# The feed-forward down projection as seven products of halves, with resident weights and stored sums of the gated values

## The chip, the cores and the metric

The kernel runs on one core of one Trainium2 chip, as one program. The metric is the device time of one execution in microseconds (us). Matrix products run on TensorE (PE; its weight loads are PEld), elementwise work on VectorE (DVE), ScalarE (ACT) and GpSimd (POOL); all DMAs of this kernel are issued by SyncE (SP). Each engine works through its own instructions in the order in which they were built, and waits on semaphores for the others.

## The reference, cut to what matters

Two layers; the part that the change touches is the feed-forward block of each (1024 tokens, D_MODEL 1024, D_FF 2816 = 22 x 128).

```python
def conv_ffn(x, w_gate, w_up, conv_w, conv_b, w_down):
    a = x @ w_gate
    u = x @ w_up
    ap = jnp.pad(a, ((0, 0), (pad, pad), (0, 0)))
    c = conv_b
    for j in range(CONV_WIDTH):
        c = c + conv_w[j] * ap[:, j:j + S]
    return (jax.nn.gelu(c) * u) @ w_down
...
        f = conv_ffn(x, ffn_w_gate[i], ffn_w_up[i], ...)
        x = layer_norm(ALPHA * x + f, ln_ffn_g[i], ln_ffn_b[i])
        x = x + jax.nn.sigmoid(x @ ple_w_gate[i]) * (p[i] @ ple_w_proj[i])
```

All of it is float32. The kernel splits each factor of a product into a high part (rounded to the PE's input type) and a low part (the rest), and adds three matmuls: high by high, low by high, high by low (`mm3`). One such matmul has a stationary operand of 128 x 128 and a moving one of 128 x 512.

## The kernel before

Tokens are held in two halves: the even ones in tiles 0 to 3, the odd ones in tiles 4 to 7, of 128 each. In a layer, the feed-forward block has two stages.

**Gate and up.** `Products` computes x @ w_gate (even m) and x @ w_up (odd m) for two blocks of 128 columns at a time, f and f + 11, so that m runs from 0 to 21 and a pair of m gives the gated values of two blocks. Each m is already made of seven products of halves (`ORDER`), of 12 matmuls each. VectorE makes the low parts of the weights (line 141) and their sums (318), adds the products up (1167), does the convolution (1236) and multiplies gate by up (1242, `times`). `spill` stores the gated block f (128 x 1024 tokens) in DRAM.

**Down.** `load(n)` fetches one block of w_down and one of the gated values, 512 KB each, and splits both: POOL rounds the weights (138), ACT the gated values (324), VectorE makes the low parts (141). `down` takes two blocks at a time (`GRP`), and for each of the 8 token tiles and 2 column halves makes 6 matmuls into a PSUM bank `pd`, which VectorE adds to the residual `xn` in SBUF (1375 the first time, with the factor ALPHA; 1378 later). That is 22 x 8 x 2 x 3 = 1056 matmuls in a layer.

```python
for n in range(0, NF, GRP):
    ...
    down([ready.pop(a) for a in range(n, n + GRP)], n == 0, before)
```

During the last two blocks `Embedding.load` brings in and splits the weights of the next matmul (`wgh`, `wgl`; low parts on VectorE and POOL in turn, line 148), normalises the first token tiles (lines 891 to 903) and turns tile 0 with 8 transposes; then the matmuls `pg` of line 158 to 160 begin.

The order on each engine is made when the program is built: a scheduler places instructions by its own estimate, within what the data, the tile buffers and some pins allow. Buffers: `unit`/`runit` come from a pool of 36 of 4 KB a partition, `rtile` from 6 of a region, `raw` from 2.

Of the kernel before, what the change touches and what calls it, by code (L numbers as in the profile page):

```python
# [8 lines left out]
F32 = mybir.dt.float32  # L9
# [3 lines left out]
ALU = mybir.AluOpType  # L13
AX = mybir.AxisListType

P = 128
# [11 lines left out]
GRP = 2  # L28
# [3 lines left out]
def tile_hybrid_encoder(  # L32
# [232 lines left out]
    gated = [dr.tile([NF, P, 1024], F32, name=f"gated{i}") for i in range(2)]  # L265
# [831 lines left out]

    class Weights:
# [123 lines left out]
    def ffn(i, w, xt, late, prefetch):  # L1222
# [21 lines left out]
        def spill(n, f):  # L1244
            nc.sync.dma_start(out=gated[i][f], in_=late_c[0][:, n, :])

        def use(pr, m, name):
# [7 lines left out]
            else:  # L1255
                if name == ("c00" if f else "c01"):
                    times(0, 0, pr.c00)
                if name == "c10":
                    times(1, 0, pr.c10)
                    times(1, 1, pr.c11)  # L1260
                    spill(1, f + nh)
                if name == "c01":
                    times(0, 1, pr.c01)
                    spill(0, f)
# [7 lines left out]

        xns = []
        fs = [f for p in range(nh) for f in (p, p + nh)]
        ready = {}

        def load(n):
            f = fs[n]
            out = []
            for dram, hi in ((w_down[i, f], nc.gpsimd), (gated[i][f], nc.scalar)):  # L1280
                v = unit("dr", [P, 1024]) if n < 2 * GRP else region[0].raw("dr", [P, 1024])
                nc.sync.dma_start(out=v, in_=dram)
                h, l = runit("dh", [P, 1024]), runit("dl", [P, 1024])
                split_value(v, h, l, hi)
                out += [h, l]
            ready[n] = out

        def before_down(j):

            if j in (0, 1):  # L1290
                load(j)
            if j in (2, 3):
                for t in range(4 * (j - 2), 4 * (j - 2) + 4):
                    xns.append(unit("xn", [P, 1024]))
                    nc.sync.dma_start(out=xns[t], in_=xmid[i][t])
            if j in (4, 5):
                load(j - 2)
# [10 lines left out]
        for n, (m, name) in enumerate(order):  # L1308
# [50 lines left out]
            if m == NF - 1:  # L1359
                before_down(Products.ORDER.index(name))  # L1360
        finished(len(order) - 1)


        def down(group, first, before=None):
            for t in range(NT):
                if before:
                    before(t)
                for n in range(2):
                    sl = slice(512 * n, 512 * n + 512)
                    po = bank("pd")  # L1370
                    for a, (wh, wl, gh, gl) in enumerate(group):
                        mm3(po, gh[:, t * P:(t + 1) * P], gl[:, t * P:(t + 1) * P], wh[:, sl], wl[:, sl],
                            a == 0, a == len(group) - 1)
                    if first:
                        nc.vector.scalar_tensor_tensor(xns[t][:, sl], xns[t][:, sl], ALPHA, po,
                                                       op0=ALU.mult, op1=ALU.add)
                    else:
                        nc.vector.tensor_tensor(xns[t][:, sl], xns[t][:, sl], po, op=ALU.add)  # L1378

        yield xns  # L1380
        before = None
        for n in range(0, NF, GRP):
            for a in range(n + 2 * GRP, n + 3 * GRP):
                if a < NF:
                    load(a)
            if n + GRP >= NF:
                before = prefetch()
            down([ready.pop(a) for a in range(n, n + GRP)], n == 0, before)


    class Embedding:
# [4 lines left out]
        def load(self):  # L1396

            for k in range(NK):
# [4 lines left out]
            def before(t):  # L1403
                if t == 2:
                    self.stats(0, False)
# [170 lines left out]
```

## Time and profile before

| | |
|---|---|
| median of 3 runs | 3108.19 us (3105.83 to 3110.84) |
| the profiled execution | 3106.23 us, its span 3104.4 us |
| PE busy | 3008.3 us (97%), mean granted clock 0.994 of full speed |
| DVE, ACT, POOL busy | 2280.5, 1186.8, 1022.9 us (73%, 38%, 33%) |
| DMA | 237.5 MB, 77 GB/s over the span |

Engines overlap, so busy times don't add up to the span. A busy time of PE counts a matmul from its start to its modelled end, and matmuls overlap in the pipeline: what one costs is read from the distance between two starts. The time beside an instruction of VectorE is likewise longer than the distance between two starts. The profiled execution lies 1.8 us outside its span, and 2.0 us under the median.

### The profile page before, as it was taken

How to read it: one execution, taken by the hardware profiler on the slowest of the kernel's cores; microseconds unless marked ns; L12 is line 12 of the kernel's file. 1: busy time of each engine (PE TensorE's matmuls, PEld its weight loads, DVE VectorE, ACT ScalarE, POOL GpSimd, SP SyncE). 2: the span in 40 equal slices, each digit the busy share in tenths (PEclk: the TensorE clock that was granted, in tenths of full speed). 3: DMA queues.
4: the chain of work that ended last, by engine and by line, in shares of the span. 5: the costliest groups of instructions: out<-in, count | busy, mean ns of one | idle time of the engine just before them, and what ended most of it. 6: DMA issues, size and time to landing. Idle time of an engine off the chain costs nothing.

```text
span 3104.4 us, 43067 instructions
## 1 busy us (share of the span) xinstructions
PE 3008.3 (97%) x15720; PEld 2582.7 (83%) x15720; DVE 2280.5 (73%) x3890; ACT 1186.8 (38%) x2538; POOL 1022.9 (33%) x1536
## 2 busy tenths in 40 slices
PE   8999999999899999999999999999998999999999
PEld 7888989887678888888888999998776888878887
DVE  6666487876898887766638777777679888877764
ACT  5555477761232222101225555555413222211111
POOL 4444534333222221101225555554223222211112
PEclk9999999999999999999999999999999999999999
DMA  3000100033222222623111000002431222243321
GB/s 121 28 28 24 33 28 8 25 126 126 85 82 82 82 82 93 220 95 109 55 59 36 32 28 28 28 24 77 156 107 68 82 82 82 82 176 136 103 77 65
DMA packets 89251, 237.52 MB, mean 77 GB/s; under 512 B 9040, under 2 KB 32720, under 8 KB 89040
## 3 DMA queue, kind: packets, MB, share of 16 engines
q1 hardware_dynamic: 89040, 234.76, 22.0%
q8 instruction: 125, 2.05, 0.3%
q14 instruction: 86, 0.70, 0.1%
HBM read 179.15 MB, written 55.57 MB: 76 GB/s over the span
## 4 chain that ended last, share of the span: by engine, by line
PE 79%; DVE 10%; DMA 3%; ACT 2%; issue 2%; POOL 2%; SPq 0%; DVEq 0%; ACTq 0%; POOLq 0%
PE pb L159 6%; PE pb L160 6%; PE pb L158 6%; PE xt L163 5%; PE pd L158 4%; PE pd L159 4%; PE pd L160 4%; PE pp L158 4%; PE pp L160 4%; PE pp L159 4%; PE s L587 4%; PE pa L158 2%; PE pa L160 2%; PE pa L159 2%; PE pg L158 2%
## 5 line engine op out<-in xcount | busy, mean ns | idle before, releaser
L141 DVE TENSOR_TENSOR ptl<-xt,pth 128x512 fp32r<-128x512 f32 (+2 forms) x384 | 239.6, 652 | 60.3 <-ACT pth L398 43.6
L158 PE MATMUL pd<-dh,dh 128*128 128x512 f32 x704 | 274.8, 390 | 3.0 <-DVE xn L1378 2.9
L1378 DVE TENSOR_TENSOR xn<-xn,pd 128x512 f32<-128x512 f32 x320 | 212.5, 683 | 87.9 <-PE pd L160 87.2
L158 PE MATMUL pp<-wh,xth 128*128 128x384 f32 x768 | 266.2, 347 | 9.7 <-ACT wh L145 7.3
L159 PE MATMUL pd<-dl,dh 128*128 128x512 f32 x704 | 274.1, 389 | 0.3 <-DVE dl L141 0.3
L160 PE MATMUL pd<-dh,dl 128*128 128x512 f32 x704 | 273.3, 389 | 0.0
L159 PE MATMUL pp<-wl,xth 128*128 128x384 f32 x768 | 259.0, 337 | 1.9 <-DVE wl L148 1.7
L160 PE MATMUL pp<-wh,xtl 128*128 128x384 f32 x768 | 258.0, 336 | 0.0
L439 ACT ACTIVATE e<-s,nmx 128x1024 f32<-128x1024 f32 x192 | 214.5, 1119 | 81.8 <-DVE nmx L837 59.0
L163 PE MATMUL xt<-ident,e 128*128 128x128 f32 x1440 | 198.8, 275 | 9.9 <-POOL e L739 3.0
L324 ACT CAST w<-ws 128x512 fp32r<-128x512 f32 x132 | 81.3, 621 | 331.6 <-PE pb L160 285.9
L158 PE MATMUL pb<-xt,w 128*128 128x512 f32 x528 | 207.1, 392 | 0.0
L159 PE MATMUL pb<-xt,w 128*128 128x512 f32 x528 | 206.9, 392 | 0.0
L160 PE MATMUL pb<-xt,w 128*128 128x512 f32 x528 | 206.7, 392 | 0.0
L163 PEld LDWEIGHTS xt<-ident,e 128*128 128x128 f32 x1440 | 164.1, 141 | 30.6 <-ACT sq L869 5.8
L138 POOL TENSOR_SCALAR w<-ws 128x512 fp32r<-128x512 f32 x44 | 32.5, 741 | 469.3 <-PE pa L160 419.0
L324 ACT CAST dh<-dr 128x1024 fp32r<-128x1024 f32 x44 | 46.1, 1052 | 335.8 <-DMA dr<-gated 202.1
L141 DVE TENSOR_TENSOR w<-ws,w 128x512 fp32r<-128x512 f32 x176 | 161.0, 918 | 4.5 <-ACT w L324 2.2
L138 POOL TENSOR_SCALAR dh<-dr 128x1024 fp32r<-128x1024 f32 x44 | 46.2, 1052 | 356.1 <-PE pd L159 168.5
L158 PEld LDWEIGHTS pd<-dh,dh 128*128 128x128 f32 x704 | 132.2, 188 | 32.7 <-DVE xn L1378 5.1
L158 PEld LDWEIGHTS pp<-wh,xth 128*128 128x128 f32 x768 | 144.6, 188 | 15.2 <-ACT wh L145 8.1
L159 PEld LDWEIGHTS pd<-dl,dh 128*128 128x128 f32 x704 | 132.2, 188 | 27.7 <-DVE dl L141 0.7
(281 smaller groups left out, 8732.4 us busy)
## 6 DMA issues: line engine op xcount, KB each, us to landing
wf<-in_w_gate_dram SPq DMA_DIRECT2D x44, 512.0 KB, 3.8
wf<-in_w_up_dram SPq DMA_DIRECT2D x44, 512.0 KB, 4.1
gated<-c SPq DMA_DIRECT2D x44, 512.0 KB, 2.8
dr<-in_w_down_dram SPq DMA_DIRECT2D x44, 512.0 KB, 3.2
dr<-gated SPq DMA_DIRECT2D x44, 512.0 KB, 3.5
wr<-in_w_c_dram SPq DMA_DIRECT2D x32, 384.0 KB, 3.3
pes<-peo SPq DMA_DIRECT2D x64, 128.0 KB, 1.9
xmid<-xn SPq DMA_DIRECT2D x16, 512.0 KB, 2.8
```

Of the source, the lines that this page charges most:

```text
L138: nc.gpsimd.tensor_scalar(o, i, 1.0, 1.0, op0=ALU.mult, op1=ALU.mult)
L141: nc.vector.tensor_tensor(lo, src, f32(hi), op=ALU.subtract)
L158: nc.tensor.matmul(o, lhsT=lh, rhs=rh, start=start, stop=False)
L159: nc.tensor.matmul(o, lhsT=lh, rhs=rl, start=False, stop=False)
L160: nc.tensor.matmul(o, lhsT=ll, rhs=rh, start=False, stop=stop)
L163: nc.tensor.transpose(o, in_=i, identity=ident)
L324: nc.scalar.copy(h, v)
L439: nc.scalar.activation(dst, s, AF.Exp, bias=negmax, scale=1.0, accum_out=l)
L587: nc.tensor.matmul(s[:, kh * 512:kh * 512 + 512], lhsT=qt[:, hl, i, :], rhs=self.ks[kh][:, j, :], start=hl == 0, stop=hl == 1)
L1378: nc.vector.tensor_tensor(xns[t][:, sl], xns[t][:, sl], po, op=ALU.add)
```

## The change

It replaces the down projection. The tokens are halved (tiles 0 to 3, 4 to 7), so are the FFN width (blocks f and f + 11) and the output columns (two of 512), and the product of the 2 x 2 halves is made from seven products (`DOWN`) instead of eight. A product sums over 11 blocks for 4 token tiles, into 4 PSUM banks that are kept over the 11 blocks. So there are 77 steps n of 4 x 3 = 12 matmuls, 924 in a layer.

- The gate and up stage also makes the four sums of gated halves (`sums_of_gated`, four passes of VectorE over 128 x 512) for each of the 11 pairs of blocks, and stores seven pieces of 128 x 512 in place of two of 128 x 1024.
- The weights of the down projection are loaded once and stay in 22 units. Their sums are made in place on VectorE (`prep`, `draw`): four passes for each f, 44 in a layer.
- Each step splits one gated piece and one weight piece of 128 x 512 (ACT and POOL the high parts, VectorE the low parts). The gated pieces come through two raw buffers, two pieces a load. The split tiles come from the 6 region buffers, two a step, so three steps stand ready at most; in the seventh product they come from the pool.
- VectorE reads the banks after each product instead of after each two blocks: 28 passes from PSUM, 8 from SBUF and 4 over 1024 columns, in place of 176 from PSUM.
- The splits of the next matmul's weights stand beside the 11 steps of the seventh product.

```diff
+DOWN = ("a00", "s4", "a01", "s2", "s3", "s1", "a11")
+AHEAD = 3
...
+    class Down:
+        B = {"a00": (0, 0), "s4": (1, 1), "a01": (1, 0), "s2": (0, 0), "s3": (1, 1), "s1": (0, 1), "a11": (1, 0)}
...
+        def load_g(self, j):
+            m = min(2, self.n - 2 * j)
+            if m > 0:
+                self.raw[j] = region[0].raw("gr", [P, 2, 512])
+                nc.sync.dma_start(out=self.raw[j][:, 0:m, :],
+                                  in_=gated[self.i][2 * j:2 * j + m].rearrange("n p q -> p n q"))
+        def draw(self, n):
...
+            if q == "s2":
+                add(b00, b11, b00)
+            if q == "s3":
+                add(b10, b10, b00, ALU.subtract)
+        def prep(self, n):
...
+            make = runit if q == "a11" else rtile
+            g, w = make("gd", [P, 2, 512]), make("wd", [P, 2, 512])
+            rg, rw = self.raw[n // 2][:, n % 2, :], self.b(f, self.B[q])
+            nc.scalar.copy(g[:, 0], rg)
+            pool_copy(w[:, 0], rw)
+            lo_part(g[:, 1], rg, g[:, 0])
+            lo_part(w[:, 1], rw, w[:, 0])
+            if q == "s4":
+                add(rw, rw, self.b(f, (0, 1)), ALU.subtract)
+            if q == "a01":
+                add(self.b(f, (0, 1)), self.b(f, (0, 1)), self.b(f, (0, 0)), ALU.subtract)
+            self.op[n] = g, w
+            if n % 2 == 1:
+                self.load_g((n + 3) // 2)
+        def product(self, n, t):
+            q, f = n // self.nh, n % self.nh
+            (g, w), ts = self.op[n], slice(t * P, t * P + P)
+            mm3(self.po[t], g[:, 0, ts], g[:, 1, ts], w[:, 0], w[:, 1], f == 0, f == self.nh - 1)
...
+        def run(self, beside):
+            nh, n_all = self.nh, self.n
+            end = n_all - AHEAD
+            for n in range(n_all):
...
+                if n < end:
+                    for t in range(4):
+                        self.product(n, t)
+                elif n == end:
+                    for t in range(4):
+                        for m in range(end, n_all):
+                            self.product(m, t)
...
+                self.draw(n + AHEAD + 2)
+                for _ in range(2):
+                    if self.todo:
+                        self.todo.pop(0)()
+                self.prep(n + AHEAD)
+                if f == nh - 1 and q < 6:
+                    self.todo += self.read(q)
+                if q == 6 and n < end:
+                    beside(f)
...
-        def spill(n, f):
-            nc.sync.dma_start(out=gated[i][f], in_=late_c[0][:, n, :])
+        def spill(name, f, v):
+            nc.sync.dma_start(out=gated[i][DOWN.index(name) * nh + f], in_=v)
+        def sums_of_gated(pr, f):
...
+            for name, o, a, b, op in (("s1", s1, a10, a11, ALU.add), ("s2", s2, s1, a00, ALU.subtract),
+                                      ("s4", s4, a01, s2, ALU.subtract), ("s3", s3, a00, a10, ALU.subtract)):
+                add(o, a, b, op)
+                spill(name, f, o)
...
+            def beside(n):
+                if n == 0:
+                    self.ln = LN(ln_fg[self.i], ln_fb[self.i])
+                    fetch(0)
+                    fetch(1)
+                if n > 0:
+                    for k in ((0,), (1,), (2,), (3, 4), (5,), (6,), (7,))[n - 1] if n <= 7 else ():
+                        fetch(k + 2)
+                        weight(k)
```

Three places of the order that results. **The first pair of the gate and up stage on VectorE**, layer 0: the end of the first gated blocks (`c`), then the weights (`ws`, `wf`, low parts `w`) and the first read of the next m (`u` from `pa`). Before:

```order
L1167 TENSOR_TENSOR u_10626<-u_10626,pb_10705 128x512
L1242 TENSOR_TENSOR c_10441<-c_10441,c_2502_10552 128x512
L1242 TENSOR_TENSOR c_10441<-c_10441,u_10626 128x512
L318 TENSOR_TENSOR ws_10744<-ws_10744,wf_10590 128x512
L141 TENSOR_TENSOR w_10754<-wf_10590,w_10754 128x512
L318 TENSOR_TENSOR ws_10745<-wf_10590,ws_10744 128x512
L141 TENSOR_TENSOR w_10771<-ws_10744,w_10771 128x512
L141 TENSOR_TENSOR w_10789<-ws_10745,w_10789 128x512
L141 TENSOR_TENSOR w_10806<-ws_10744,w_10806 128x512
L1167 TENSOR_TENSOR u_10774<-m_10757,pa_10731 128x512
```

and now, in the same place:

```order
L1330 TENSOR_TENSOR u_10626<-u_10626,pb_10705 128x512
L1405 TENSOR_TENSOR c_10441<-c_10441,c_2502_10552 128x512
L1405 TENSOR_TENSOR c_10441<-c_10441,u_10626 128x512
L319 TENSOR_TENSOR c_2502_10552<-c_10441 128x512
L319 TENSOR_TENSOR c_2464_10384<-c_10441 128x512
L319 TENSOR_TENSOR u_10626<-c_2502_10552,c_10441 128x512
L319 TENSOR_TENSOR ws_10753<-ws_10753,wf_10590 128x512
L319 TENSOR_TENSOR u_10626<-c_10441,u_10626 128x512
L319 TENSOR_TENSOR ws_10754<-wf_10590,ws_10753 128x512
L142 TENSOR_TENSOR w_10763<-wf_10590,w_10763 128x512
L142 TENSOR_TENSOR w_10780<-ws_10753,w_10780 128x512
```

The four sums of gated halves (line 319 into `c`, `c`, `u`, `u`) stand ahead of the weights and of the next read.

**The middle of the down stage on VectorE.** Before, the low parts `dl` of whole blocks stand between the reads of the banks:

```order
L141 TENSOR_TENSOR dl_13615<-dr_13612,dh_13614 128x1024
L1378 TENSOR_TENSOR xn_13499<-xn_13499,pd_13816 128x512
L141 TENSOR_TENSOR dl_13621<-dr_13618,dh_13620 128x1024
L1378 TENSOR_TENSOR xn_13501<-xn_13501,pd_13824 128x512
L1378 TENSOR_TENSOR xn_13501<-xn_13501,pd_13832 128x512
L1378 TENSOR_TENSOR xn_13517<-xn_13517,pd_13840 128x512
```

Now, from the low parts of step 11 (`wd_13866`, `gd_13865`) to those of step 13:

```order
L142 TENSOR_TENSOR wd_13866<-wd_13683,wd_13866 128x512
L142 TENSOR_TENSOR gd_13865<-gr_13787,gd_13865 128x512
L319 TENSOR_TENSOR wd_13683<-wd_13683,wd_13536 128x512
L319 TENSOR_TENSOR wd_13536<-wd_13536 128x512
L319 TENSOR_TENSOR wd_13536<-wd_13683,wd_13536 128x512
L142 TENSOR_TENSOR gd_13888<-gr_13829,gd_13888 128x512
L142 TENSOR_TENSOR wd_13889<-wd_13705,wd_13889 128x512
L319 TENSOR_TENSOR wd_13705<-wd_13705,wd_13538 128x512
L319 TENSOR_TENSOR wd_13538<-wd_13538 128x512
L142 TENSOR_TENSOR gd_13909<-gr_13829,gd_13909 128x512
L142 TENSOR_TENSOR wd_13910<-wd_13725,wd_13910 128x512
```

The sums of weights (line 319), which the source spreads over four products, stand close together: 39 of the 44 lie between the low parts of step 11 and those of step 28, and 4 reads of banks with them.

**The end of the down stage on POOL.** Before, the four low parts of the next weights follow the last rounding of a down block:

```order
L138 TENSOR_SCALAR dh_14830<-dr_14828 128x1024
L148 TENSOR_TENSOR wgl_15105<-wgr_15102,wgh_15104 128x1024
L148 TENSOR_TENSOR wgl_15117<-wgr_15114,wgh_15116 128x1024
L148 TENSOR_TENSOR wgl_15129<-wgr_15126,wgh_15128 128x1024
L148 TENSOR_TENSOR wgl_15141<-wgr_15138,wgh_15140 128x1024
L895 TENSOR_SCALAR rs_15183<-mv_15182 128x1
```

Now they stand among the last roundings (`wd`, of steps 71 to 76):

```order
L139 TENSOR_SCALAR wd_15141<-wd_13789 128x512
L149 TENSOR_TENSOR wgl_15151<-wgr_15098,wgh_15150 128x1024
L139 TENSOR_SCALAR wd_15169<-wd_13809 128x512
L139 TENSOR_SCALAR wd_15203<-wd_13831 128x512
L149 TENSOR_TENSOR wgl_15213<-wgr_15148,wgh_15212 128x1024
L896 TENSOR_SCALAR rs_15184<-mv_15183 128x1
L897 TENSOR_TENSOR rs_15184<-rs_15184,mhalf 128x1
L139 TENSOR_SCALAR wd_15235<-wd_13851 128x512
L149 TENSOR_TENSOR wgl_15243<-wgr_15210,wgh_15242 128x1024
L139 TENSOR_SCALAR wd_15262<-wd_13874 128x512
L139 TENSOR_SCALAR wd_15294<-wd_13895 128x512
L149 TENSOR_TENSOR wgl_15300<-wgr_15240,wgh_15299 128x1024
```

So the roundings of steps 72, 74 and 75 stand behind one of these passes each.

## Rows read from the trace of the kernel before

**Rows 1.** The page: busy time by engine, and the chain that ended last.

```profile
PE 3008.3 (97%) x15720; PEld 2582.7 (83%) x15720; DVE 2280.5 (73%) x3890; ACT 1186.8 (38%) x2538; POOL 1022.9 (33%) x1536
...
PE 79%; DVE 10%; DMA 3%; ACT 2%; issue 2%; POOL 2%; SPq 0%; DVEq 0%; ACTq 0%; POOLq 0%
```

**Rows 2.** Stretches: length, busy time by engine (instructions), granted clock, DMA share, GB/s.

```profile
845.00:860.00 15.00, 10.72 (x36) 8.43 (x37) 14.38 (x21) 5.56 (x8) 3.26 (x3) 0.67 0.00 1
...
875.00:900.00 25.00, 23.31 (x101) 18.99 (x102) 24.71 (x37) 8.96 (x13) 7.85 (x7) 1.00 0.26 86
960.00:1245.00 285.00, 285.00 (x1246) 232.51 (x1245) 228.17 (x321) 80.55 (x115) 72.53 (x70) 1.00 0.24 85
1245.00:1488.00 243.00, 241.24 (x1065) 198.82 (x1065) 177.12 (x237) 31.74 (x31) 32.07 (x28) 1.00 0.38 131
```

**Rows 3.** PE in order of time, both down stages: start, us, line, names.

```profile
1245.05 0.39 PE L158 MATMUL pd<-dh,dh 128*128 128x512 f32 x1
...
1268.85 0.39 PE L158 MATMUL pd<-dh,dh 128*128 128x512 f32 x1
...
1484.42 1.04 PE L163 MATMUL xt<-ident,xn 128*128 128x128 f32 x8
...
1488.04 0.39 PE L158 MATMUL pg<-wgh,xth 128*128 128x512 f32 x1
...
2760.12 0.39 PE L158 MATMUL pd<-dh,dh 128*128 128x512 f32 x1
...
3003.08 0.39 PE L158 MATMUL pg<-wgh,xth 128*128 128x512 f32 x1
```

**Rows 4.** VectorE in order of time, passes of 128 x 512 that follow each other.

```profile
929.23 0.68 DVE L318 TENSOR_TENSOR ws<-ws,wf 128x512 f32<-128x512 f32 x1
929.94 1.66 DVE L318 TENSOR_TENSOR ws<-wf,ws 128x512 f32<-128x512 f32 x1
...
1239.86 0.68 DVE L1167 TENSOR_TENSOR m<-m,pb 128x512 f32<-128x512 f32 x1
1240.46 0.68 DVE L1167 TENSOR_TENSOR c<-u,pb 128x512 f32<-128x512 f32 x1
```

**Rows 5.** VectorE and POOL in order of time where both work.

```profile
893.71 1.17 POOL L138 TENSOR_SCALAR w<-wf 128x512 fp32r<-128x512 f32 x1 [0.46 <-PE pb L160]
893.72 0.68 DVE L1242 TENSOR_TENSOR c<-c,c 128x512 f32<-128x512 f32 x1
894.32 1.09 DVE L318 TENSOR_TENSOR ws<-ws,wf 128x512 f32<-128x512 f32 x1
895.34 0.67 DVE L1167 TENSOR_TENSOR m<-m,pb 128x512 f32<-128x512 f32 x1
```

**Rows 6.** PE after its waits early in the gate and up stage, layer 0.

```profile
849.28 0.77 PE L158 MATMUL pa<-xb,w 128*128 128x512 f32 x1 [9.17 <-DVE u L1167]
849.84 0.63 PE L159 MATMUL pa<-xb,w 128*128 128x512 f32 x1
850.27 0.63 PE L160 MATMUL pa<-xb,w 128*128 128x512 f32 x1
...
875.51 0.50 PE L158 MATMUL pb<-xb,w 128*128 128x512 f32 x1 [1.41 <-DVE u L1167]
875.85 0.40 PE L159 MATMUL pb<-xb,w 128*128 128x512 f32 x1
```

**Rows 7.** By tile: durations (ns min/median/max) of splits on VectorE and POOL.

```profile
L148 DVE TENSOR_TENSOR wgl<-wgr,wgh x8: 1224/1226/1525, 1427.2 to 2962.0; 128x1024 fp32r<-128x1024 f32 x8
L148 POOL TENSOR_TENSOR wgl<-wgr,wgh x8: 2393/2398/2410, 1429.8 to 2967.1; 128x1024 fp32r<-128x1024 f32 x8
...
L138 POOL TENSOR_SCALAR w<-ws x44: 612/619/2029, 831.1 to 2729.0; 128x512 fp32r<-128x512 f32 x44
```

**Rows 8.** VectorE by line and shape, 825 to 1245 us: busy, mean ns.

```profile
L141 DVE TENSOR_TENSOR w<-ws,w 128x512 fp32r<-128x512 f32 x85 | 78.5, 928 | 1.2 <-POOL w L138 0.5
...
L318 DVE TENSOR_TENSOR ws<-wf,ws 128x512 f32<-128x512 f32 x20 | 21.6, 1078 | 0.6
```

**Rows 9.** DMA issues: KB each, median us from issue to landing.

```profile
dr<-gated SPq DMA_DIRECT2D x44, 512.0 KB, 3.5
```

More of the change, by code (lines that the diff above doesn't have):

```diff
@@ L264, in tile_hybrid_encoder @@
     xmid = [dr.tile([NT, P, 1024], F32, name=f"xmid{i}") for i in range(2)]
-    gated = [dr.tile([NF, P, 1024], F32, name=f"gated{i}") for i in range(2)]
+    gated = [dr.tile([7 * NF // 2, P, 512], F32, name=f"gated{i}") for i in range(2)]
     def transposed(xn, put):
@@ L1098, in tile_hybrid_encoder, with residual @@
+    def residual(i, xns, t):
+        xns.append(unit("xn", [P, 1024]))
+        nc.sync.dma_start(out=xns[t], in_=xmid[i][t])
     class Weights:
@@ L1260, in use @@
                     times(1, 1, pr.c11)
-                    spill(1, f + nh)
+                    spill("a01", f, late_c[0][:, 1, 0:512])
+                    spill("a11", f, late_c[0][:, 1, 512:1024])
                 if name == "c01":
                     times(0, 1, pr.c01)
-                    spill(0, f)
+                if name in ("c01", "c10") and not any(x in ("c01", "c10") for x, _ in pr.sums if x != name):
+                    sums_of_gated(pr, f)
         def finished(n):
@@ L1273, in ffn @@
         xns = []
[L1274 to L1297, printed above, removed]
+        down = Down(i, xns)
         pr = [Products(w[m], xt) for m in range(NF)]
@@ L1359, in ffn @@
             if m == NF - 1:
-                before_down(Products.ORDER.index(name))
+                down.ahead(Products.ORDER.index(name))
         finished(len(order) - 1)
[L1364 to L1378, printed above, removed]
-        yield xns
[L1381 to L1388, printed above, removed]
+        yield xns
+        down.run(prefetch())
     class Embedding:
@@ L1396, in load, with fetch, weight @@
         def load(self):
-            for k in range(NK):
-                self.w.append(load_split(w_ple[self.i, k], [P, 1024], "wg", rtile if k < 3 else runit, nc.scalar,
-                                         nc.gpsimd if k % 2 else nc.vector))
-            self.ln = LN(ln_fg[self.i], ln_fb[self.i])
-            def before(t):
-                if t == 2:
+            raw = {}
+            def fetch(k):
+                if k < NK:
+                    raw[k] = unit("wgr", [P, 1024])
+                    nc.sync.dma_start(out=raw[k], in_=w_ple[self.i, k])
+            def weight(k):
+                make = rtile if k < 3 else runit
+                h, l = make("wgh", [P, 1024]), make("wgl", [P, 1024])
+                split(raw.pop(k), h, l, nc.scalar, nc.gpsimd if k % 2 else nc.vector)
+                self.w.append((h, l))
+            def beside(n):
[7 more added lines that the diff above has]
+                        weight(k)
+                if n == 3:
                     self.stats(0, False)
-                if t == 5:
+                if n == 5:
                     self.apply(0)
-                if t == 6:
+                if n == 6:
                     self.stats(1, False)
-                if t == 7:
+                if n == 7:
                     self.turn(0)
-            return before
+            return beside
         def stats(self, t, pin=True):
```

87 lines of the change are left out of this document (86 added, 1 removed).

## The prediction

> **What bounds the kernel now.** I first read engine shares and the chain of waits. PE is busy 97% of the span and makes up 79% of the chain; VectorE comes next with 73% busy and 10% of the chain [rows 1]. Shares are means, so I then read the two stages that change as stretches. In a steady part of gate and up, PE is busy in all of 285.00 us and VectorE in 228.17; in the down stage of layer 0 PE is busy 241.24 of 243.00 us, VectorE 177.12, the DMA engines .38 of the time, at full granted clock [rows 2]. So the down stage is bound by TensorE's instruction count, with a quarter of VectorE free. The question is whether VectorE, which gets the work that pays for fewer products, still delivers each split tile in time.
>
> The pitch of a matmul comes from the list of starts, not from the 0.39 us beside it: 105 matmuls lie between 1245.05 and 1268.85, so 23.80/105 = 0.2267 us [rows 3]. The down stage lasts 1488.04 − 1245.05 = 242.99 us in layer 0 and 3003.08 − 2760.12 = 242.96 in layer 1, from the first `pd` to the first `pg`. Of this 1056 × .2267 = 239.4 is matmuls, 1.0 the eight transposes [rows 3], and 2.6 us waiting.
>
> **What it removes.** 1056 − 924 = 132 matmuls a layer, 132 × .2267 = 29.9 us, 59.8 for both. They lie on the path itself. The 2.6 us of waiting belong to the old loop and go with it (5.2); the waits of the new one are counted anew. A new down stage without any wait would last 924 × .2267 + 1.0 = 210.5 us, and the program 3106.2 − 65.0 = 3041.2.
>
> **Gate and up: what is added.** Four sums for each of 11 pairs are 44 passes of 128 x 512, at 0.60 us from start to start (1240.46 − 1239.86, [rows 4]): 2.4 us a pair. A pair of m is 14 products × 12 × .2267 = 38.1 us, so 285 us hold 7.5 pairs, and VectorE's idle 56.8 us [rows 2] are 7.6 us a pair: steady pairs hide the 2.4. The first pair doesn't. There VectorE is busy 24.71 of 25.00 us [rows 2], and PE waits 1.41 us at 875.51 for a `u` of VectorE [rows 6]; the sums stand in VectorE's queue ahead of the next weights' low parts and of the next `u`, and PE waits for both. So 2.4 us go straight onto the path. Ends: 0, if they fall into a gap, and 4.4, if the POOL copies of the weights collide with each of them (below). The stores move from two to seven a pair, of 256 KB against 512, hence 1.75 MB against 1; nobody waits for them before the down stage, and the DMA share there is .24 [rows 2]. I take nothing.
>
> **The price of a collision.** POOL's rounding of a weight piece takes 0.62 us alone [rows 7]. At 893.71 it took 1.17 beside a VectorE pass with both operands in SBUF, and VectorE's next such pass took 1.09 instead of .68, its successor starting 1.02 us later (895.34 − 894.32) instead of .60 [rows 5]. A POOL rounding among such passes therefore costs VectorE .42; I count one for each. The Trainium skill, "SBUF — State Buffer", section "Who interferes with whom", says that VectorE's second SBUF input and GpSimd share a port pair, which one holds for a whole instruction while the other is fully blocked. By it a rounding would cost its whole 0.62, .20 more than measured, which with the 25 roundings counted below would be 5 us a layer more, 3082 in place of my sum; the row decides here, and the sum uses .42.
>
> **Down, steps 12 to 28 (stretch A).** The order places 39 of the 44 weight sums here. VectorE's queue holds in these 17 steps: 34 low parts × .60 = 20.4; 39 sums × .66 (between .60 and the .71 = 929.94 − 929.23 of a sum that takes the one before as its operand, [rows 4]; most here are in chains) = 25.7; 4 reads of banks × .60 = 2.4; 17 roundings on POOL × .42 = 7.1. That is 55.6 us. PE needs 17 × 12 × .2267 = 46.2. The split tiles come from six buffers, so VectorE can be about 3.4 us ahead: tiles come free at the end of a step, are needed two steps (5.44 us) later, and take about 2.0 to fill (a rounding of .62 and two low parts, with some slack between). PE so waits 55.6 − 46.2 − 3.4 = 6.0 us a layer. Ends: 0 with no collision and .60 throughout (46.2 against 46.2), and, if the passes cost what their group means say in gate and up, 928 ns a low part and 1078 a sum [rows 8], 34 × .93 + 39 × 1.08 + 2.4 = 76.1, so 76.1 − 49.6 = 26.5 us. These means hold longer work of POOL beside them (its sums of weights), which this stretch doesn't have; hence I stay near [rows 4, 5].
>
> **Down, steps 66 to the last group (stretch B).** From the first read of the sixth product's banks (2.0 us before step 66) to the low parts of the last step VectorE has 8 reads and 16 low parts, 24 × .60 = 14.4; 4 `wgl` × 1.23 = 4.9 [rows 7]; and of the normalisation two passes over 1024 and four half rows of statistics, 2 × 1.23 + 4 × .60 = 4.9: 24.2 us. PE gives it 2.0 + 8 × 2.72 + 1.0 of transposes + 6 × .2267 = 26.2, since the last split tile is wanted six matmuls into the last group. POOL adds 8 roundings (3.4), and three `wgl` of 2.40 us [rows 7], each of which collides longer: at about 2.2 (its length less the gaps) 6.6. So VectorE needs 34.2, 8.0 more than there is. Some of POOL's work will fall beside the reads of banks, which take only one operand from SBUF, so I take 6.0 a layer, ends 0 and 8.0. Before, the four `wgl` of POOL stood behind the last rounding and delayed no split tile; now the roundings of steps 72, 74 and 75 stand behind one each.
>
> **DMA.** The gated pieces come through two buffers of two pieces, refilled when VectorE and ACT have finished the pair. A load then has about 3 × 2.72 − 2.0 − .3 = 5.8 us to land; one of the same 512 KB took a median of 3.5 [rows 9]. Nothing, with 2.3 us to spare. SyncE issues them in order, with the residual's and the next weights' loads between, which are few. ACT's rounding of the gated pieces, and its one copy of banks, find it idle most of the time (31.74 busy of 243, [rows 2]): nothing.
>
> **Sum.** −59.8 − 5.2 + 2 × (2.4 + 6.0 + 6.0) = −36.2. 3106.2 − 36.2 = 3070.0 for a profiled execution; the median lies 2.0 above it, so 3072. The added waits would have to reach 65.0/2 = 32.5 us a layer for the gain to vanish.
>
> **Rivals.**
> 1. *Nearly the full gain.* The scheduler's lead is larger than I think, or collisions rarer: VectorE's idle quarter takes it all. 0 to 7 us of waits a layer: 3043 to 3057 as a median, 3050 in the middle. For it: VectorE's passes without POOL beside them just fit stretch A (46.2). Against: PE waited for VectorE wherever VectorE was full [rows 6]. Chance .20.
> 2. *VectorE becomes the bound of stretch A,* at the means of [rows 8]: 26.5 + 6.0 + 2.4 = 34.9 us a layer, so 3106.2 − 65.0 + 69.8 + 2.0 = 3113. The band from 3092 to 3114 is this case in part or whole. For it: these means are this kernel's own, for the same operations and shapes. Against: what lengthens them stands beside them in gate and up, not here. Chance .14.
> 3. *Slower: TensorE's clock falls in stretch A.* At 849.28, after 9.17 us of idling, matmuls started .43 apart (849.84 to 850.27), the 1.2 GHz level, and the granted clock of those 15 us was .67 [rows 6, 2]. If short waits before each of 17 steps brought that level, the steps would take 17 × 12 × .20 = 41 us more, 6 of it in place of the waits: 35 a layer, 3072 + 70 = 3142. It decides from about half the stretch at the low level on, where the gain of 36 is gone in both layers. Against it: after the 1.41 us wait at 875.51 the next start came .34 later and the stretch kept clock 1.00 [rows 6, 2]. The Trainium skill, "TensorE: Matmul & The Clock Gate", section "A second HAM failure mode: psum-queue depth-cycling", tells of a kernel whose frequent micro-idles between groups of matmuls made the clock swing between its levels; the 875 stretch here, with waits and full clock, speaks against it for idles of this size. Chance .06.
> 4. *Others:* the ring of gated pieces becomes the bound (it would need landings of about 9.8 us throughout to undo the gain), or waits in places that I haven't costed. Chance .04, most of it slower.
>
> **How the numbers follow.** My forecast, waits of 7 to 25 us a layer (3057 to 3092), has .56; the others are as above. The range for 8 in 10 leaves out the lowest part of rival 1 (under 3046, about .05), the top of rival 2 (over 3106, .05), rival 3 and the others: 3046 to 3106. A measurement of this kernel can tell about 0.2%, 6.2 us, from no change: below 3102 is faster, above 3114 slower. Faster: .20 + .56 + .05 of rival 2 + .01 = .82. The same: .09 of rival 2. Slower: .06 + .03 = .09.
>
> **What would show it.** The new profile should have 1848 matmuls into `pd`; the time from the first `pd` to the first `pg` should be about 222 us a layer (210.5 + 12), full clock throughout. PE's waits there should name the low parts `gd` or `wd` of VectorE, and lie in steps 12 to 28 and around the last group; POOL's roundings should be longer than .62 there and low parts longer than .68. In the first pair of gate and up PE's waits for `u` or `w` should grow by about 2.4 us. If the stage takes 210 to 213 us, rival 1 is right and collisions were overpriced; if waits fill stretch A and low parts average .9 us, rival 2; a granted clock below .95 there is rival 3. I am wrong in the working, even at a right total, if ACT, a gated load or a bank read is what PE waits for.

## The result and the profile after

The changed kernel takes 3074.64 us (median; 3070.20 to 3077.26), the kernel before on the same chip 3107.16 (3105.83 to 3110.84): a ratio of 0.9892, 95% interval 0.9875 to 0.9909, so 1.1% less. The forecast was 3072 with a range of 3046 to 3106. The profiled execution, span 3068.4 us against 3104.4, is the quickest of the four runs; the stage lengths below are from it.

The page of the changed kernel, the lines that answer to [rows 1] and [rows 9]:

```profile
PE 2956.1 (96%) x15456; PEld 2535.4 (83%) x15456; DVE 2339.5 (76%) x4014; ACT 1239.0 (40%) x2652; POOL 1110.6 (36%) x1646
...
PE 70%; DVE 16%; issue 6%; POOL 3%; ACT 3%; DMA 2%; SPq 0%; POOLq 0%; DVEq 0%; ACTq 0%
...
L160 PE MATMUL pd<-wd,gd 128*128 128x512 f32 x616 | 242.4, 393 | 4.2 <-DVE wd L142 4.2
...
gr<-gated SPq DMA_DIRECT2D x76, 512.0 KB, 3.7
```

3 x 616 = 1848 matmuls go into `pd`, as planned. PE's share of the chain of waits fell from 79% to 70%, and VectorE's rose from 10% to 16%: the work saved on TensorE was partly given back as waits for VectorE. The stretches say where (length, then busy time of PE, PEld, DVE, ACT, POOL, granted clock, DMA share, GB/s; compare [rows 2]):

```profile
845.00:860.00 15.00, 11.23 (x39) 8.84 (x40) 14.38 (x22) 5.88 (x8) 3.77 (x3) 0.71 0.00 1
875.00:900.00 25.00, 22.59 (x92) 18.33 (x93) 23.12 (x36) 7.82 (x11) 8.26 (x7) 0.93 0.23 85
960.00:1245.00 285.00, 283.63 (x1239) 230.98 (x1238) 241.73 (x350) 81.08 (x117) 70.74 (x70) 1.00 0.32 110
1293.00:1325.00 32.00, 30.33 (x128) 23.09 (x126) 31.48 (x49) 6.76 (x11) 12.92 (x11) 1.00 0.49 178
1430.00:1471.00 41.00, 33.98 (x146) 28.00 (x145) 38.89 (x45) 15.98 (x20) 18.08 (x13) 0.92 0.53 198
```

In the two stretches of the down stage that the prediction named, VectorE is full (31.48 of 32, 38.89 of 41) and PE is not. PE in order of time in the down stage of layer 0, its first matmul, two of its waits, and the end (start, us, line, names, and in brackets the idle time and what ended it; compare [rows 3]):

```profile
1248.09 0.39 PE L159 MATMUL pd<-wd,gd 128*128 128x512 f32 x1
...
1300.70 0.50 PE L160 MATMUL pd<-wd,gd 128*128 128x512 f32 x1 [0.51 <-DVE wd L142]
...
1328.45 0.50 PE L160 MATMUL pd<-wd,gd 128*128 128x512 f32 x1 [0.40 <-DVE wd L142]
...
1460.65 1.97 PE L164 MATMUL xt<-ident,xn 128*128 128x128 f32 x8 [7.02 <-DVE xn L904]
1462.28 0.78 PE L159 MATMUL pd<-wd,gd 128*128 128x512 f32 x1
1462.85 0.63 PE L160 MATMUL pd<-wd,gd 128*128 128x512 f32 x1
1463.28 0.63 PE L161 MATMUL pd<-wd,gd 128*128 128x512 f32 x1
...
1471.71 0.39 PE L159 MATMUL pg<-wgh,xth 128*128 128x512 f32 x1
```

The stage lasts 1471.71 − 1248.09 = 223.62 us (before 242.99). Waits, here and below, are what the distances between starts have over .2267 us for a matmul (.13 for a transpose), summed where it is more than .03 us, so that a slow clock behind a wait counts with it:

| stretch | layer 0 | layer 1 | forecast |
|---|---|---|---|
| gate and up, from the matmul after the long wait to the first `pd` | 395.77 to 399.32 us | 395.61 to 397.99 us | +2.4 |
| down stage | 242.99 to 223.62 us | 242.96 to 225.17 us | 222.5 |
| of it waits in steps 12 to 33 | 3.84 | 3.78 | 6.0 |
| of it waits in steps 74 to 76 | 9.00 | 10.54 | 6.0 |

These stretches give 31.2 of the 36.0 us. The other 4.8 lie where the change does nothing, 4.6 of them between the layers, from the first `pg` to the matmul after the next long wait, which lasts 876.5 us before, 871.9 here, and 874.1 to 876.1 in the first eight kernels below. I take them for this run's luck; the medians lie 32.5 apart.

### The profile page after: what moved, and what is told of

Same layout as the page of the kernel before. It is cut to its first block, busy times and chain, and to the rows that moved or that the text cites. A ratio compares the mean times of both kernels' runs of the same rounds, so it can differ in the third digit from the quotient of the medians.

```text
span 3068.4 us, 43192 instructions
## 1 busy us (share of the span) xinstructions
PE 2956.1 (96%) x15456; PEld 2535.4 (83%) x15456; DVE 2339.5 (76%) x4014; ACT 1239.0 (40%) x2652; POOL 1110.6 (36%) x1646
## 4 chain that ended last, share of the span: by engine, by line
PE 70%; DVE 16%; issue 6%; POOL 3%; ACT 3%; DMA 2%; SPq 0%; POOLq 0%; DVEq 0%; ACTq 0%
PE xt L164 5%; PE pb L159 5%; PE pb L160 5%; PE pb L161 5%; PE pp L159 4%; PE s L588 4%; PE pp L161 4%; PE pp L160 4%; PE pd L160 2%; PE pd L161 2%; PE pd L159 2%; PE pa L159 2%; PE pg L159 2%; PE pa L161 2%; PE pa L160 2%
## 5 line engine op out<-in xcount | busy, mean ns | idle before, releaser
L160 PE MATMUL pd<-wd,gd 128*128 128x512 f32 x616 | 242.4, 393 | 4.2 <-DVE wd L142 4.2
L159 PE MATMUL pd<-wd,gd 128*128 128x512 f32 x616 | 241.0, 391 | 0.0
L161 PE MATMUL pd<-wd,gd 128*128 128x512 f32 x616 | 240.5, 390 | 0.0
L139 POOL TENSOR_SCALAR wd<-wd 128x512 fp32r<-128x512 f32 x154 | 129.9, 848 | 290.8 <-PE pd L161 215.6
L1149 ACT CAST gd<-gr 128x512 fp32r<-128x512 f32 x154 | 94.8, 622 | 312.2 <-PE pd L161 222.0
L142 DVE TENSOR_TENSOR wd<-wd,wd 128x512 fp32r<-128x512 f32 x154 | 112.3, 731 | 68.8 <-POOL wd L139 68.8
L142 DVE TENSOR_TENSOR w<-ws,w 128x512 fp32r<-128x512 f32 x176 | 152.4, 869 | 5.2 <-ACT w L325 3.2
L838 DVE TENSOR_REDUCE nmx<-s 128x1 f32<-128x1024 f32 x128 | 150.4, 1213 | 1.7 <-PE s L588 1.6
L159 PE MATMUL pb<-xb,w 128*128 128x512 f32 x352 | 140.2, 398 | 9.8 <-DVE u L1330 5.7
```

The lines of the kernel that those rows point to most:

```text
L139: nc.gpsimd.tensor_scalar(o, i, 1.0, 1.0, op0=ALU.mult, op1=ALU.mult)
L142: nc.vector.tensor_tensor(lo, src, f32(hi), op=ALU.subtract)
L159: nc.tensor.matmul(o, lhsT=lh, rhs=rh, start=start, stop=False)
L160: nc.tensor.matmul(o, lhsT=lh, rhs=rl, start=False, stop=False)
L161: nc.tensor.matmul(o, lhsT=ll, rhs=rh, start=False, stop=stop)
L838: nc.vector.tensor_reduce(out=nmx, in_=s, axis=AX.X, op=ALU.max, negate=True)
```

## Experiments

The theory is that of the prediction: the saving is 65.0 us less what PE waits for VectorE at three places, and GpSimd's passes make these waits longer. All kernels were timed beside the kernel before, and the ratios are to it (the changed kernel has 0.9892); experiments 5 and 6 have one execution each and no ratio.

**1. Roundings of the down weights on ScalarE.**

```diff
-            pool_copy(w[:, 0], rw)
+            nc.scalar.copy(w[:, 0], rw)
```

> The changed kernel with one edit: the weight pieces of the down stage are rounded on ScalarE instead of GpSimd (154 roundings a layer-pair moved; nothing left out). Theory (VectorE's queue plus .42 us for each collision with a rounding on GpSimd): in steps 12 to 28 PE's waits fall from 3.8 us a layer to under 1, since VectorE then needs 48.5 us where it has 49.6; around the last group they fall from 8.4 and 10.0 us by about 3.4 (8 roundings); in all about 7 us a layer, 14 us in the program, to about 3060. Rival (VectorE is full there by its own passes, or the low parts wait for chains of sums in place): waits stay at 3.8 and 8.4 to 10, the time at 3074.

3062.74 us, ratio 0.9849 (0.9834 to 0.9863). Waits in steps 12 to 33: 0 in both layers. Around the last group 6.5 and 7.7 us, 2.6 and 2.9 less. The same passes of VectorE from 1280 to 1328 us (group, count, busy, mean ns), of the changed kernel:

```profile
L319 DVE TENSOR_TENSOR wd<-wd,wd 128x512 f32<-128x512 f32 x25 | 18.2, 761 | 0.0
L142 DVE TENSOR_TENSOR wd<-wd,wd 128x512 fp32r<-128x512 f32 x16 | 12.5, 783 | 0.5 <-POOL wd L139 0.5
L142 DVE TENSOR_TENSOR gd<-gr,gd 128x512 fp32r<-128x512 f32 x16 | 10.9, 679 | 0.0
L319 DVE TENSOR_TENSOR wd<-wd 128x512 f32<-128x512 f32 x10 | 8.3, 848 | 0.1
```

and of this one:

```profile
L319 DVE TENSOR_TENSOR wd<-wd,wd 128x512 f32<-128x512 f32 x29 | 18.9, 683 | 0.1
L142 DVE TENSOR_TENSOR gd<-gr,gd 128x512 fp32r<-128x512 f32 x18 | 12.3, 684 | 0.0
L142 DVE TENSOR_TENSOR wd<-wd,wd 128x512 fp32r<-128x512 f32 x18 | 12.3, 683 | 0.0
L319 DVE TENSOR_TENSOR wd<-wd 128x512 f32<-128x512 f32 x10 | 6.8, 685 | 0.1
```

No pass is lengthened any more, and more of them fit (75 against 67). VectorE is still full there, with .2 us of idle time in the 48, but it is no longer late. So the rival falls, by which its own passes would make PE wait.

**2. The same roundings twice on GpSimd.**

```diff
             pool_copy(w[:, 0], rw)
+            pool_copy(w[:, 0], rw)
```

> The changed kernel with every rounding of a down weight piece made twice on GpSimd, the second with the same result over the first. Theory (.42 us of VectorE for each rounding beside passes with two SBUF operands): 17 more roundings add 7.1 us a layer in steps 12 to 28, waits there 3.8 to about 11, and about 3.4 us around the last group; the steps between hide them, as VectorE is three quarters busy; about 21 us in all, 3095. By a lock for the whole instruction (.62 each) 10.5 and 5 us a layer, 31 us in all, 3105. Rival (GpSimd's roundings cost VectorE nothing): at most the rounding's latency, under 2 us a layer, 3077.

3101.87 us, ratio 0.9976 (0.9966 to 0.9985). Waits in steps 12 to 33: 11.16 and 11.03, so 7.32 and 7.25 us for 17 roundings more, .43 us each (.41 if step 29, where the last of these waits lies, is counted as an eighteenth): the price taken from [rows 5], and not .62. Around the last group 12.7 and 11.2; 2.3 and 2.6 elsewhere, most at steps 60 and 65, which the expectation had as hidden. The time is 27 us above the changed kernel's where 21 were expected, nearer to the 31 of a full lock; the waits of steps 12 to 28, where VectorE is full throughout, and not the total tell the two prices apart.

**3. Twenty-two weight sums spread.**

```diff
             if q == "s2":
-                add(b00, b11, b00)
+                tc.keep_in_program_order(nc.vector.tensor_tensor(b00, b11, b00, op=ALU.add))
             if q == "s3":
-                add(b10, b10, b00, ALU.subtract)
+                tc.keep_in_program_order(nc.vector.tensor_tensor(b10, b10, b00, op=ALU.subtract))
```

> The changed kernel with the 22 weight sums of the fourth and fifth product pinned to the program's order, so that VectorE makes them one a step in steps 34 to 52 and not in 16 to 33; nothing left out. Theory (too much work for VectorE in steps 12 to 28): some 25 sums instead of 39 stand there, 34 low parts, 25 sums and 4 reads at .61 and 17 collisions at .42 are 46 us, less than the 49.6 it has: waits 3.8 to about 0, no new ones in steps 34 to 52; 3.8 us a layer, about 7.5 in all, 3067. Rival (a low part waits for the rounding on GpSimd or the buffers, whatever VectorE's load): waits unchanged, 3074.

3068.60 us, ratio 0.9866 (0.9850 to 0.9883). The interval overlaps that of the changed kernel; the waits tell the two apart. In steps 12 to 33 they are .21 and .22, and there are no new ones. The roundings stay on GpSimd here: either fewer sums or no collisions end the waits, as a queue that is over its limit by a few us demands. The last group is as it was (9.49 and 10.43).

**4. All low parts of the next weights on VectorE.**

```diff
-                split(raw.pop(k), h, l, nc.scalar, nc.gpsimd if k % 2 else nc.vector)
+                split(raw.pop(k), h, l, nc.scalar, nc.vector)
```

> The changed kernel with all eight low parts of the next weights (wgl) on VectorE, none on GpSimd; nothing left out. Theory (each pass of 2.4 us on GpSimd holds VectorE up by about 2.2 us, where VectorE itself would need 1.2): the three in the stretch before the last group cost 3.6 in place of 6.6 us, PE's waits around the last group fall from 8.4 and 10.0 to about 5.5 and 7; about 6 us in all, 3068. Rival (VectorE's own work is what fills the stretch, collisions are small): 3.6 us a layer more, waits of 12 and 13.5, 3082.

3062.51 us, ratio 0.9845 (0.9830 to 0.9860). Waits around the last group 2.67 and 3.76: 6.3 and 6.8 us less, twice the expected 3. VectorE does four passes more and is ready sooner, so the rival falls. VectorE and GpSimd of the changed kernel show why; first VectorE:

```profile
1438.66 1.71 DVE L142 TENSOR_TENSOR gd<-gr,gd 128x512 fp32r<-128x512 f32 x1
...
1442.51 2.29 DVE L142 TENSOR_TENSOR gd<-gr,gd 128x512 fp32r<-128x512 f32 x1
...
1450.15 3.41 DVE L149 TENSOR_TENSOR wgl<-wgr,wgh 128x1024 fp32r<-128x1024 f32 x1
1453.48 1.09 DVE L142 TENSOR_TENSOR gd<-gr,gd 128x512 fp32r<-128x512 f32 x1
1454.49 1.09 DVE L142 TENSOR_TENSOR wd<-wd,wd 128x512 fp32r<-128x512 f32 x1
1455.51 3.35 DVE L903 TENSOR_TENSOR xn<-xn,lngb 128x1024 f32<-128x1024 f32 x1
...
1459.39 1.21 DVE L904 TENSOR_TENSOR xn<-xn,lngb 128x1024 f32<-128x1024 f32 x1
```

and GpSimd:

```profile
1437.00 2.82 POOL L149 TENSOR_TENSOR wgl<-wgr,wgh 128x1024 fp32r<-128x1024 f32 x1 [7.84 <-ACT wgh L146]
1439.78 2.09 POOL L139 TENSOR_SCALAR wd<-wd 128x512 fp32r<-128x512 f32 x2
1441.84 2.40 POOL L149 TENSOR_TENSOR wgl<-wgr,wgh 128x1024 fp32r<-128x1024 f32 x1
...
1449.64 2.83 POOL L149 TENSOR_TENSOR wgl<-wgr,wgh 128x1024 fp32r<-128x1024 f32 x1
1452.45 2.60 POOL L139 TENSOR_SCALAR wd<-wd 128x512 fp32r<-128x512 f32 x2
1455.02 2.77 POOL L149 TENSOR_TENSOR wgl<-wgr,wgh 128x1024 fp32r<-128x1024 f32 x1
```

Four passes of GpSimd lie there, not three; 1.03 + 1.61 + 2.20 + 2.14 = 7.0 us of VectorE's time goes into them beside .68 or 1.21 for the passes held up. In experiment 4 three of the four moved passes stand ahead of line 904, 1.14 us each from start to start, so that 3.6 us are saved; fewer held-up low parts and less idle time save .7 more. And the wait that is left is short enough to spare 2.1 us of slow transposes and matmuls behind it, which were 2.2 in the changed kernel (1.97 − 1.04, and six matmuls .2 late). That makes 6.4 us, beside the 6.3 measured in layer 0.

**5. The transposes behind the first half of the last group.** Only the place of `turn(0)` in the program differs.

```diff
-                    self.turn(0)
+                    return lambda: self.turn(0)
...
                             for step in self.read(q)[0:2]:
                                 step()
+                            late()
```

> The changed kernel with the eight transposes of tile 0 placed behind the first half of the last group of 36 matmuls instead of ahead of the group; nothing left out. Theory (VectorE's whole queue in steps 69 to 76 is late, the low parts of steps 75 and 76 as well as the normalised tile): PE starts the last group some 5 to 7 us earlier and then stands at its first tokens for the low parts of steps 75 and 76; the down stage stays at 223.6 and 225.2 us, within 1. Rival (only the normalisation of tile 0 is late, so its place in PE's order is the whole cost): the waits fall by 6 us or more a layer, to a stage of 216 to 218.

One execution, 3082.77 us. PE in order of time (layer 0, the down stage begins at 1250.59):

```profile
1458.90 0.50 PE L160 MATMUL pd<-wd,gd 128*128 128x512 f32 x1 [2.51 <-DVE wd L142]
...
1464.53 0.80 PE L160 MATMUL pd<-wd,gd 128*128 128x512 f32 x1 [4.67 <-DVE wd L142]
...
1467.54 0.80 PE L160 MATMUL pd<-wd,gd 128*128 128x512 f32 x1 [1.35 <-DVE wd L142]
```

PE now stands for low parts three times, those of steps 74, 75 and 76. The rival falls: VectorE's whole queue is late, not the one tile. That the stage would be the same within 1 us was wrong too: 226.43 and 227.87 us, 2.8 and 2.7 longer. Behind the second and the third wait the matmuls start .43 us apart, behind the first they don't; what else adds to it I haven't separated.

**6. The first pair's sums of gated halves left out.**

```diff
-                add(o, a, b, op)
-                spill(name, f, o)
+                if f:
+                    add(o, a, b, op)
+                spill(name, f, o if f else a)
```

> The changed kernel without the four sums of gated halves in the first pair of blocks of each layer (the first pair's stored sums are plain halves instead; the sums of the other ten pairs stay). Theory (the four passes ahead of the next weights and reads in VectorE's full queue are what the first pair lost): from the first matmul after the long wait of 9.2 us to the first of the down stage 396 us in both layers, as before the change (395.8 and 395.6), against 399.3 and 398.0 with the sums; PE's wait of 2.87 us back to about 1.4; at most 1 us left over in layer 0 from small waits in later pairs. Rival (the seven stores a pair or GpSimd's work cost it): stays at 398 to 399.

One execution, 3069.53 us. From the matmul after the long wait to the first `pd` it is 396.95 and 395.82 us; PE's wait in the first pair is 1.42 us again (2.87 with the sums). The four passes account for at most 2.4 of the 3.55 us in layer 0 and 2.2 of the 2.38 in layer 1: 1.9 and 1.8 of this in the first two pairs, the rest in later pairs, which the edit leaves as they are. What stays in layer 0 are mostly small waits for ScalarE's `m` in later pairs.

**7 and 8. Edits 1, 3 and 4 together; and with the first sums put off** (called at the next pair's `c11` instead of at once).

> The changed kernel with the edits of the first, third and fourth experiment together (roundings of down weights on ScalarE, the 22 sums spread, all low parts of the next weights on VectorE). Theory: no waits in steps 12 to 28; around the last group the 2.7 and 3.8 us of the fourth experiment less the roundings' collisions (the third to the sixth pass there, 1 to 1.5 us), so 1 to 2.5 us; down stage 212 to 213 us, the gate and up stage unchanged at 398 to 399; in all 2 x 11.5 = 23 us less than the changed kernel, about 3051. Rival (ScalarE, with two roundings a step and the next weights' too, becomes late in steps 66 to 76): waits of PE for low parts whose cause is ScalarE, 4 us or more a layer, 3060 or above.

> As the one before, and the sums of the first pair of gated blocks are put off until the next pair's first products have been read. Theory: from the first matmul after the long wait to the down stage falls from 399.3 and 398.0 to about 396.5, so 4 us less than the one before in all, about 3047. Rival (the four passes only move into a queue that is as full): 398 to 399 stays, 3051.

Together: 3048.38 us, ratio 0.9809 (0.9793 to 0.9826); down stage 211.57 and 211.79 us, waits 1.2 and 1.4. ScalarE is not late, so the rival falls. With the sums put off: 3046.09 us, ratio 0.9801 (0.9787 to 0.9816), which the intervals don't tell apart; gate and up 398.91 and 398.59 against 399.62 and 398.80. PE's wait in the first pair shrank from 2.8 to 2.0 us, and waits of .3 to .7 for `m` came at the next pairs: the rival holds, the passes moved into a queue that is as full.

**9 and 10. In these two kernels the gate and up weights are rounded on ScalarE too.**

```diff
-        HI = {"s3", "a01", "a11"}
+        HI = set()
```

> The combined kernel (roundings of down weights on ScalarE, spread sums, next weights' low parts on VectorE), and the roundings of gate and up weights on ScalarE as well, so that GpSimd rounds no weight beside VectorE; nothing left out. Theory (.42 us of VectorE for each rounding, where VectorE is full): three roundings of GpSimd stand ahead of PE's wait of 2.8 us in the first pair, so that it falls by about 1.3 to 1.5 us a layer; in the steady pairs they are hidden; gate and up 399.6 and 398.8 become about 398, in all 2 to 3 us, 3046. Rival (ScalarE gets three more roundings an m there and is late with its copy m, for which PE already waits .2 to .9 us at some pairs): more such waits, gate and up 400 or above, 3050 or more.

> The same edit in the kernel whose first sums of gated halves are put off. Theory: with three collisions fewer the put-off sums find 1.3 us more room: 398.9 and 398.6 become about 397.5, in all 2 to 3 us less than without, 3044. Rival: ScalarE's copies m are late, as above, 3048 or more.

3033.84 us, ratio 0.9757 (0.9743 to 0.9772), and 3033.78, ratio 0.9759 (0.9743 to 0.9776). That is 14.5 us where 2 to 3 were expected. PE in the kernel of experiment 9, after its long wait:

```profile
843.92 0.77 PE L159 MATMUL pa<-xb,w 128*128 128x512 f32 x1 [6.13 <-DVE u L1330]
```

The wait of 9.17 us of [rows 6], which all kernels so far had, is 6.13 here. The expectation had reckoned only with what lies behind it. Ahead of it GpSimd's roundings stand beside VectorE's splits of tokens (the kernel of experiment 7, VectorE):

```profile
833.68 2.10 DVE L142 TENSOR_TENSOR w<-ws,w 128x512 fp32r<-128x512 f32 x2 [0.52 <-POOL w L139]
835.71 1.63 DVE L319 TENSOR_TENSOR c<-c,xb 128x1024 f32<-128x1024 f32 x1
837.26 1.63 DVE L319 TENSOR_TENSOR c<-xb,t 128x1024 f32<-128x1024 f32 x1
```

Without them (experiment 9) the two passes into `c` take what a pass of that size does alone:

```profile
831.53 1.21 DVE L319 TENSOR_TENSOR c<-c,xb 128x1024 f32<-128x1024 f32 x1
832.67 1.22 DVE L319 TENSOR_TENSOR c<-xb,t 128x1024 f32<-128x1024 f32 x1
```

Behind the wait, gate and up fell to 395.08 and 394.84 us, 4.5 and 4.0 less, where 1.3 to 1.5 were expected. PE's waits for ScalarE's `m` fell from 1.7 and 1.0 us in experiment 7 to .6 and .1, so the rival falls. Putting the first sums off gains nothing on top of it (394.97 and 394.92 us).

**11. The same edit alone in the kernel before.**

> The kernel before the change, with the roundings of gate and up weights on ScalarE instead of GpSimd; nothing left out, the down projection is the old one. Theory (the roundings held VectorE up at the start of gate and up in both kernels, so what the ninth experiment gave has nothing to do with the change): PE's wait of 9.17 us falls to about 6.1, the first pair's waits of 1.4 and 1.2 us shrink, some 6 to 8 us a layer, 3107 to about 3094. Rival (the gain comes only where the new sums of gated halves fill VectorE's queue): at most 2 us, 3106.

3095.67 us, ratio 0.9956 (0.9940 to 0.9973), near the expected 3094. PE after its waits early in gate and up, to be read beside [rows 6]:

```profile
844.13 0.77 PE L158 MATMUL pa<-xb,w 128*128 128x512 f32 x1 [6.12 <-DVE u L1167]
...
869.17 0.50 PE L158 MATMUL pb<-xb,w 128*128 128x512 f32 x1 [0.20 <-DVE u L1167]
...
879.00 0.50 PE L158 MATMUL pa<-xt,w 128*128 128x512 f32 x1 [1.82 <-ACT m L1177]
```

The long wait is 6.12 us, so these 3 us a layer have nothing to do with the down projection. Behind it the rival is right: the first pair's wait for `u` falls from 1.41 to .20 us, but the next one, for ScalarE's `m`, grows from 1.18 to 1.82 with a slower clock behind it. Gate and up takes 396.33 and 396.44 us, .6 and .8 more than in the kernel before. So the 4.5 and 4.0 us that experiment 9 won behind the wait come only where the sums of gated halves fill VectorE's queue. The long waits and what follows them give about 5 of the 10.8 us between the two profiled executions; the rest lies where the edit does nothing, and I can't tell it from a run's luck. By the medians, with the edit in both, the change and its own three repairs stand at .9757/.9956 = .980. Whether the old down stage would gain from its roundings on ScalarE wasn't tried.

## Why the prediction was right

**What it removes.** 924 matmuls a layer are left, 1848 in all. The stages of experiment 7, 211.57 and 211.79 us, less their waits of 1.2 and 1.4 are 210.4: the 210.5 us and the 65.0 us of the sum stand.

**Gate and up.** +2.4 us a layer was forecast, all of it in the first pair; measured +3.55 and +2.38. The four passes in the first pair's full queue are a cause, as experiment 6 shows, but the first two pairs lost only 1.7 and 1.8 us. PE's wait for `u` grew from 1.41 to 2.87 us, by 1.46 and not by 2.4. The matmuls behind it started .43 us apart, which cost 1.7 us:

```profile
877.41 0.62 PE L159 MATMUL pb<-xb,w 128*128 128x512 f32 x1 [2.87 <-DVE u L1330]
877.83 0.63 PE L160 MATMUL pb<-xb,w 128*128 128x512 f32 x1
878.26 0.63 PE L161 MATMUL pb<-xb,w 128*128 128x512 f32 x1
```

In exchange, a wait for ScalarE's `m` that PE had further on is gone; this is the kernel before:

```profile
884.69 0.50 PE L158 MATMUL pa<-xt,w 128*128 128x512 f32 x1 [1.18 <-ACT m L1177]
```

The other 1.8 and .6 us lie in the nine pairs behind, partly in waits of .2 to .6 us for `m`: the steady pairs don't hide their sums wholly. That layer 1 came out at the forecast 2.4 is luck.

**Stretch A.** Place, cause and price were right; the size was not: 6.0 expected, 3.84 and 3.78 measured. PE waited from step 19 to 28 only, five or six times, and the granted clock stayed at 1.00 there. The price of a rounding is .43 us (experiment 2). The mis-sized term is the .66 us for a sum. I had read .71 for a sum behind the one that it takes its operand from [rows 4], but the order puts another pass between most of these pairs: in experiment 1 sums and low parts alike have means of 683 to 685 ns and lie .60 us from start to start. 39 x .06 = 2.3 us, the size of the difference; the lead of 3.4 us wasn't tested by itself.

**Stretch B.** 6.0 expected, 9.00 and 10.54 measured. The sum came near and the step behind it failed. By the sum, VectorE needs 34.2 us from the first read of a bank to the last low part and has 26.2, so it is 8.0 us late; I then took 6.0. It needed 32.7 us in both layers and had 24.3 and 22.8 (up to where PE would have wanted that low part, had it not waited from step 66 on), so it was 8.3 and 9.9 us late. VectorE of the changed kernel at both ends of the stretch in layer 0, and with ScalarE at its start in layer 1:

```profile
1430.92 0.69 DVE L142 TENSOR_TENSOR gd<-gr,gd 128x512 fp32r<-128x512 f32 x1 [0.63 <-ACT gd L1149]
1431.53 0.68 DVE L1180 TENSOR_TENSOR xn<-xn,pd 128x512 f32<-128x512 f32 x1
...
1463.58 0.63 DVE L142 TENSOR_TENSOR wd<-wd,wd 128x512 fp32r<-128x512 f32 x1
...
2925.28 1.14 ACT L1149 CAST gd<-gr 128x512 fp32r<-128x512 f32 x2 [6.09 <-DMA gr<-gated]
2925.93 0.69 DVE L142 TENSOR_TENSOR gd<-gr,gd 128x512 fp32r<-128x512 f32 x1 [2.16 <-ACT gd L1149]
```

Four of its terms were wrong and partly made each other good. The first read comes .2 us ahead of step 66 in layer 0 and 1.4 behind its start in layer 1, not 2.0 ahead. I counted two long passes of the normalisation, and VectorE makes the third too (line 904, 1.1 us). I counted three passes of GpSimd, and four lie there; as two of them fell in part beside reads of banks, as I had argued, they cost 7.0 us and not four times 2.2. And only three of the eight roundings held VectorE up (1.2 us for 3.4).

I let PE wait for the low parts of the last step, and it waited first for the transposes' input, `xn` of line 904. That changes little: experiment 5 says that the low parts were late as well, so that mending the order alone gains nothing. For the same reason the 2.2 us of slow clock behind the wait, which I had left out, add only about .7 us: PE would else have waited for the low parts of step 76.

**DMA, ScalarE.** Loads of `gr` land in 3.7 us, those of before in 3.5 [rows 9]; PE never waited for one itself, or for a read of a bank. But nothing was too little for this term. In layer 1 VectorE stood 2.16 us for ScalarE's rounding of a gated piece whose load took 5.1 us to land, and .63 us in layer 0, where that load took 3.6. Its queue so began 1.5 us later, and 1.5 us is what PE waits longer in layer 1 (10.54 against 9.00); no run tests this by itself.

**The rivals.** The full gain (rival 1) needed 0 to 7 us of waits a layer; 16 to 17 came. Rival 2's means stood beside longer work of GpSimd, as argued. Of the low parts of [rows 8], 59 had no GpSimd work beside them in the trace of the kernel before and took 683 ns in the mean, and 18 beside its sums of weights took 1723. In stretch A the means were 679 to 848 ns, against 928 and 1078 in [rows 8]. Rival 3 stays away: clock 1.00 in 1293 to 1325 us despite the repeated waits of .4 to .5, and in 1285 to 1325 us of experiment 2 despite waits of 1.2. After the 7.02 us wait the clock was at the 1.2 GHz level (matmuls .43 apart). The Trainium skill, "TensorE: Matmul & The Clock Gate", section "A second HAM failure mode: psum-queue depth-cycling", tells of frequent short idles between groups of matmuls that make the clock swing. No run here shows that for repeated waits of up to 1.2 us.

**Small slips in the sums.** 2.4 + 4 × .42 is 4.1 and not 4.4, 26.2 is 26.1, and how rival 4 comes to 9.8 us isn't worked out; none moves the forecast.

The forecast lay 2.6 us under the median because the errors have both signs: −2.2 a layer in A, +3.0 and +4.5 in B, +1.2 once in gate and up. That more than half of B's error was made good in A is luck; the places, the cause and the 65.0 us are not. The 4.8 us that the profiled run won elsewhere are not in the median.

## What to carry to other kernels

When products are traded for sums, cost the sums at the engine that makes them, in the stretches where that engine is already full. Count such a stretch from when its first input has landed, and list everything that the engine makes up to the last thing that the waiting engine wants of it. Before believing that VectorE is full, see who works beside it: here the change gave 1.1% with GpSimd rounding weights, and with ScalarE doing it and two more repairs 2.4%, of which .4% was the old kernel's to have.

## What the runs showed of the hardware

GpSimd beside VectorE costs VectorE GpSimd's own time less about .2 us, for short and long passes alike: .43 us for a rounding of .62 (experiment 2), and 2.14 to 2.20 for a pass of 2.40 [rows 7] in the rows of experiment 4 that were held up from the start. VectorE's passes with two operands in SBUF stand still meanwhile: 3.41 us for one that takes 1.21 alone. The Trainium skill, "SBUF — State Buffer", section "Who interferes with whom", calls the port pair that the two share an exclusive lock, held for a whole instruction. The rows agree but for the .2 us. The prediction had set the .42 against that rule; the long passes, which it priced at 2.2 and which cost 2.14 to 2.20, fit the rule with the same .2 us off.

The wait of 2.87 us in the first pair was followed by matmuls .43 us apart in layer 0, 1.7 us in all; the one of 1.41 us before [rows 6] and one of 2.51 us in experiment 5 by none. So the sums' 1.46 us of longer wait cost more than themselves there; the first two pairs lose only 1.7 us in all because the later wait for `m` went.
